# A Hyena, S5 and ConvGLU block: transfers moved, x normalised in two halves, gate sums in 16 steps

## The chip, the cores and the metric

One core of one Trainium2 chip. The metric is the device time of one execution in microseconds (us). The engines are named as in the profile: PE (matrix products), DVE (vector), ACT (activation), POOL (general), SP (here it only issues transfers).

## The reference

One layer (DEPTH 1, D_MODEL 1024, 1024 tokens, a context of 256 tokens) in fp32:

```
pc = modulated_norm(ctx, norm_g[l, 0], mod_c[0], mod_c[1]) @ w_in[l]
yc_s5, ctx_state = s5_mixer(pc[..., h_split:], *s5_args, None, not last)

px = modulated_norm(x, norm_g[l, 0], mod_x[0], mod_x[1]) @ w_in[l]
yx_s5, _ = s5_mixer(px[..., h_split:], *s5_args, ctx_state, True)
yx_hy = hyena_mixer(px[..., :h_split], *hyena_args)
yx = jnp.concatenate([yx_hy, yx_s5], axis=-1) @ w_out[l]
x = x + mod_x[2] * rms_norm(yx, norm_g[l, 1])
hx = modulated_norm(x, norm_g[l, 2], mod_x[3], mod_x[4])
x = x + mod_x[5] * rms_norm(conv_glu_ffn(hx, rows, *ffn_args), norm_g[l, 3])
```

The six rows of `mod_x` are `silu(c) @ w_ada + b_ada`: shifts, scales and gates of 1024 columns each. `hyena_mixer` is a short convolution, a long convolution by FFT (four channel tiles of 128 here) and a gate. `s5_mixer` is a bidirectional diagonal state space model whose output passes a GELU and then a GLU, `y * sigmoid(y @ w_glu + b_glu)`.

## The kernel before

Nearly all products keep fp32 precision as three products of split operands (`mm3`, lines 228 to 230). A scheduler orders PE, DVE and ACT, except where program order is pinned; transfers issued by SP (`ld`, line 152) keep program order, POOL's work too. Lines 143, 149 and 161 are helpers that record DVE's and POOL's two-operand operations and ACT's activations, so instructions of many places carry them.

**Start, 0 to 48 us.** Eight steps k multiply the conditioning by the first two rows of `w_ada` (`ada_mm`, line 308), 1 MB each. From step 4 on each also squares one of the four tiles `xr` of x (two token blocks each) on ACT, with a sum per token. After the loop `norm(2, 8)` turns the eight sums into factors (a square root on ACT, small DVE instructions) and `apply` scales the four tiles on DVE. The row of products is copied (`mrow`), transposed on PE (line 592), and DVE makes the coefficients `AB`, `A0` of it. `k_load(0)` and `ld(Cb)` load tables; the first filter taps are products at line 445.

**Projections of x, to 204 us.** `Cc[1]` is negated on ACT as soon as its table `k_c` has come. `w_split(i)` splits weight tiles into a high and a low part, `x_cols(k)` transposes x on PE (line 648) and applies scale and shift on ACT (the high part), then DVE (the low part), and `x_mm` multiplies.

**S5 turns, 204 to 432 us and beyond.** A loop over n = 0 to 8 does S5 batch n in pieces (`s5_u`, `s5_gt`, `s5_kc`, `s5_e`, `s5_scan_a`, `s5_toep`, `s5_scan_b` for turn n, `s5_out` for n−1). Between the pieces `hy_next` does pieces of the Hyena projections and `sums_next(MS[i])` steps of the generator `gate_sums`: the remaining four rows of `w_ada`, in steps of 128 columns. One step loads 512 KB into the single buffer `wm`, issues eight narrow products into a PSUM bank (line 691, 32 output partitions), copies them to SBUF on ACT, sums partitions with a short product (line 693), and adds the bias on ACT. After each row's last step `gate_end` makes the scale, or transposes the row and writes it to memory `g_d`. `MS = (1, 2, 2, 1, 1)` gives seven steps a turn, and four in the last.

**End of S5, 500 to 614 us.** The long convolution of channel tile ct is `u_spec(ct)` (forward FFT, PE and DVE), `product(ct)` with the filter's spectrum `kf` on DVE, and `inverse(ct)`: `fft_inv` on DVE, products with the table `idft` on PE (line 1078), and the gate on DVE. The S5 output was written to memory `ys_d` by ACT's queue and is read back as `ys4`, in another layout. The GLU (`glu_w`, `glu_y`, `glu_high` at line 1187, `glu_low` at line 1195) works on pairs of 128 output channels: a sigmoid on ACT into the one buffer `sg`, a multiplication by it on DVE. Then come `inverse(1)` to `inverse(3)`, and `wo_load`, `wo_split`: `w_out`, whose products begin at 613.5 us. The FFN follows.

Of the kernel before, what the change touches and what calls it, by code (L numbers as in the profile page):

```python
# [108 lines left out]
def hybrid_block(ctx: ExitStack, tc: tile.TileContext, t, out):  # L109
# [19 lines left out]
    def FRing(n, *dims, at=None):  # L129
        return Ring(sa, n, *dims, at=at)  # L130
# [29 lines left out]
    def act(o, i, f, **k):  # L160
        return pin(A, A.activation(o, i, f, **k))  # L161
# [355 lines left out]
    def norm(o, n):  # L517
        rstd(nrs[:, o:o + n], nss[:, o:o + n], ntmp[:, :, o:o + n])
# [61 lines left out]
    norm(2, 8)  # L580
    for q in range(4):
        apply(V, xr[q], 2 + 2 * q)
# [76 lines left out]
    def gate_end(i, b0):  # L659

        if i == 4:
            stt(V, A2, SB2[:, 1], 1.0, g2v, ADD, MUL)
        if i in (2, 5):
            z = 2 + (i == 5)
            tt(V, SB2[:, z], SB2[:, z], g13[:, z - 2], MUL)
            PE.transpose(PS[:8, b0, 0:128], SB2[:, z], ident)
            act(macc[:8], PS[:8, b0, 0:128], AF.Copy)
            ld(g_d[z - 2][0].rearrange("(k c) -> k c", k=8), macc[:8])
# [3 lines left out]
    def gate_sums(gates, wm, acc, b0):  # L672

        steps = [(i, h) for i in gates for h in range(8)]
        ws_ = {}

        def load(n):
            if n < len(steps):
                i, h = steps[n]
                ws_[n] = wm.next()  # L680
                c0 = i * 1024 + 128 * h
                ld(ws_[n].rearrange("p (k c) -> p k c", k=8),
                   w_ada[:, c0:c0 + 128].rearrange("(k p) c -> p k c", p=128))

        load(0)
        for n, (i, h) in enumerate(steps):
            w = ws_.pop(n)
            w3_ = w.rearrange("p (k c) -> p k c", k=8)
            for k in range(8):
                j = k % 4  # L690
                PE.matmul(PS[32 * j:32 * j + 32, b0[0], 0:128], lhsT=cond[:, k], rhs=w3_[:, k], start=k < 4, stop=k >= 4)  # L691
            act(acc, PS[:, b0[0], 0:128], AF.Copy)
            PE.matmul(PS[:, b0[0], 128:130], lhsT=acc, rhs=sel, start=True, stop=True)
            z, bias = {3: (0, b34[:, 0:8]), 4: (1, b34[:, 8:16]), 2: (2, b25[:, 0:8]), 5: (3, b25[:, 8:16])}[i]
            act(SB2[:, z, h:h + 1], PS[:, b0[0], 128:129], AF.Identity, bias=bias[:, h:h + 1])
            if h == 7:
                gate_end(i, b0[0])
            load(n + 1)
            yield

    g_d = [drp.tile([1, 1024], F32, name=f"g{i}_d") for i in range(2)]
    macc = F(128, at=(0,))
# [37 lines left out]
    act(Cc[1], Cc[1], AF.Copy, scale=-1.0)  # L740
    w_split(0)
    x_cols(0)
    for k in range(8):
        i = k // 2
        if k % 2:
            w_split(i + 1)
        if k < 7:
            x_cols(k + 1)
        disc_next(D0[k])
        k_next(K0[k])  # L750
        x_mm(i, k, 0)
# [5 lines left out]
    sums = gate_sums((3, 4, 2, 5), wm, macc, gb)  # L757
# [39 lines left out]
    for k in range(8):  # L797
# [4 lines left out]
        sums_next(M_WIN)  # L802
# [229 lines left out]
    s5_load(0)  # L1032

# [49 lines left out]
    for n in range(9):  # L1083
# [5 lines left out]
        if n == 5:  # L1089
            sums_next(48)  # L1090
            wm.put()
            sa.put(macc)
# [71 lines left out]
    graw, sg = F(2, 512, at=(7,)), F(1024, at=(7,))  # L1164
    xin = FRing(2, 1024, at=(7,))
# [65 lines left out]
    sa.put(graw, sg, yh, *yl, *gw)  # L1231
# [242 lines left out]
MS, UF = (1, 2, 2, 1, 1), 1  # L1474
# [107 lines left out]
```

## Time and profile before

| what | before |
|---|---|
| runs | 1447.63 us median of 3 (1445.07 to 1448.21) |
| profiled execution | 1447.4 us, its span 1445.6 us |
| PE busy | 1326.1 us (92%), 6668 instructions |
| DVE busy | 883.5 us (61%), 1208 instructions |
| ACT busy | 482.3 us (33%), 802 instructions |
| POOL busy | 472.5 us (33%), 250 instructions |
| mean granted clock of PE | 0.951 |
| moved by DMA | 144.48 MB, mean 100 GB/s |

The span runs from the first to the last instruction of the profiled execution. Idle time in a row stands in brackets with what ended it. PE's instructions overlap: one product of 512 columns lasts 0.39 us in the rows, and the next begins 0.23 us after it.

### The profile page before, as it was taken

Reading aid. Unit: us, or ns where it says so; the run is one execution under the profiler, and the core shown is the slowest. Engines: PE = TensorE matmul, PEld = TensorE weight load, DVE = VectorE, ACT = ScalarE, POOL = GpSimd, SP = SyncE. Lnnn points to the kernel's source line nnn. Section 1 sums busy time; section 2 is a strip of 40 time slices with the busy share of each in tenths; the row PEclk is TensorE's granted clock in tenths of the full one; section 3 lists DMA queues with packets and bytes.
Section 4 is the critical chain, followed back from the end, with each engine's and each line's share of the span. In section 5 each row is a group of like instructions: output and inputs, shape, how many; then the busy total and the mean of one; then the engine's idle time right before and its main releaser. Section 6 shows DMA issues by size and latency. Waiting matters only on the chain.

```text
span 1445.6 us, 16905 instructions
## 1 busy us (share of the span) xinstructions
PE 1326.1 (92%) x6668; PEld 1071.5 (74%) x6668; DVE 883.5 (61%) x1208; ACT 482.3 (33%) x802; POOL 472.5 (33%) x250
## 2 busy tenths in 40 slices
PE   4888789899989957899999999999999999999997
PEld 0666567677767855787778888888888888888886
DVE  7776842456677999647766755755756757115314
ACT  3632122444433413346633222222222233224321
POOL 0000726556589203210122222222222226443540
PEclk8799899989998887999999999999999999999999
DMA  9423143545533225213311111111111115335422
GB/s 376 143 96 102 66 94 93 163 138 154 156 94 109 74 83 209 73 58 114 124 44 44 49 54 44 46 57 44 45 57 44 44 58 171 107 101 176 132 73 88
DMA packets 149639, 144.48 MB, mean 100 GB/s; under 512 B 29860, under 2 KB 128696, under 8 KB 147128
## 3 DMA queue, kind: packets, MB, share of 16 engines
q1 hardware_dynamic: 135000, 124.67, 27.9%
q10 hardware_dynamic: 14560, 18.74, 3.7%
q8 instruction: 52, 0.85, 0.2%
q14 instruction: 27, 0.22, 0.1%
HBM read 123.98 MB, written 19.37 MB: 99 GB/s over the span
## 4 chain that ended last, share of the span: by engine, by line
PE 73%; DVE 16%; DMA 5%; ACT 3%; issue 2%; SPq 1%; ACTq 0%; DVEq 0%
PE PS L228 21%; PE PS L229 21%; PE PS L230 21%; DVE s L143 12%; ACT s L161 3%; DMA s<-in_w_ada_dram 2%; DVE s L149 1%; PE PS L691 1%; PE PS L972 1%; DVE s L1001 1%; PE PS L428 1%; DMA s<-in_x_dram 1%; PE PS L936 1%; PE PS L429 1%; PE PS L1078 1%
## 5 line engine op out<-in xcount | busy, mean ns | idle before, releaser
L228 PE MATMUL PS<-s,s 128*128 128x512 f32 x1320 | 527.6, 401 | 4.2 <-ACT s L161 3.9
L229 PE MATMUL PS<-s,s 128*128 128x512 f32 x1320 | 524.1, 397 | 0.0
L230 PE MATMUL PS<-s,s 128*128 128x512 f32 x1320 | 523.1, 397 | 0.1
L161 ACT ACTIVATE s<-s 128x512 fp32r<-128x512 f32 (+9 forms) x356 | 259.6, 748 | 641.0 <-PE PS L229 208.2
L143 POOL TENSOR_TENSOR s<-s,s 128x1024 fp32r<-128x1024 f32 x98 | 252.2, 2577 | 613.5 <-ACT s L161 593.5
L143 DVE TENSOR_TENSOR s<-s,s 128x512 fp32r<-128x512 f32 (+6 forms) x178 | 196.8, 1117 | 218.7 <-ACT s L161 210.4
L143 POOL TENSOR_TENSOR s<-s 128x512 f32<-128x512 f32 (+2 forms) x147 | 219.0, 1503 | 262.4 <-PE PS L445 145.7
L228 PEld LDWEIGHTS PS<-s,s 128*128 128x128 f32 x1320 | 258.2, 196 | 59.9 <-ACT s L161 6.4
L230 PEld LDWEIGHTS PS<-s,s 128*128 128x128 f32 x1320 | 258.0, 196 | 53.8 <-issue 2.7
L229 PEld LDWEIGHTS PS<-s,s 128*128 128x128 f32 x1320 | 258.8, 196 | 52.5 <-issue 2.6
L149 DVE SCALAR_TENSOR_TENSOR s<-s,s 128x1024 f32<-128x1024 f32 x140 | 218.0, 1557 | 102.5 <-ACT s L161 98.3
L143 DVE TENSOR_TENSOR s<-s 128x512 f32<-128x512 f32 (+11 forms) x403 | 187.0, 500 | 41.9 <-DMA s<-s 27.1
L161 ACT ACTIVATE s<-PS 128x512 f32<-128x512 f32 (+6 forms) x212 | 110.8, 538 | 227.1 <-PE PS L429 53.2
L149 DVE SCALAR_TENSOR_TENSOR s<-s 128x1024 f32<-128x1024 f32 (+5 forms) x136 | 107.6, 807 | 54.9 <-ACT s L161 52.5
L161 ACT ACTIVATE s<-PS,s 128x128 f32<-128x128 f32 (+5 forms) x161 | 101.9, 680 | 81.7 <-PE PS L230 18.5
L143 DVE TENSOR_TENSOR s<-PS,s 128x512 f32<-128x512 f32 (+3 forms) x81 | 52.4, 668 | 62.5 <-ACT s L161 24.4
L230 PE MATMUL PS<-s 128*128 128x512 f32 x136 | 53.7, 395 | 0.0
L228 PE MATMUL PS<-s 128*128 128x512 f32 x136 | 53.4, 395 | 0.0
L229 PE MATMUL PS<-s 128*128 128x512 f32 x136 | 53.4, 392 | 0.0
L149 DVE SCALAR_TENSOR_TENSOR s<-PS,s,s 128x1023 f32<-128x1023 f32 x24 | 30.6, 1278 | 26.4 <-ACT s L161 25.9
L1078 PE MATMUL PS<-s,s 128*128 128x256 f32 x128 | 31.2, 406 | 15.6 <-DMA s<-in_k_idft_dram 14.8
L1078 PEld LDWEIGHTS PS<-s,s 128*128 128x128 f32 x128 | 26.1, 205 | 20.2 <-DVE s L143 16.1
(89 smaller groups left out, 803.0 us busy)
## 6 DMA issues: line engine op xcount, KB each, us to landing
s<-in_ffn_w_up_dram SPq DMA_DIRECT2D x44, 512.0 KB
s<-in_ffn_w_down_dram SPq DMA_DIRECT2D x44, 512.0 KB
s<-in_w_ada_dram SPq DMA_DIRECT2D x32, 512.0 KB
s<-in_w_in_dram SPq DMA_DIRECT2D x20, 512.0 KB
s<-in_w_ada_dram SPq DMA_DIRECT2D x8, 1024.0 KB
s<-in_x_dram SPq DMA_DIRECT2D x4, 1024.0 KB
kf_d<-s ACTq DMA_DIRECT2D x4, 1024.0 KB
s<-kf_d SPq DMA_DIRECT2D x4, 1024.0 KB
```

What stands on the lines that cost most here:

```text
L143: return pin(e, e.tensor_tensor(o, a, b, op=op))
L149: return pin(e, e.scalar_tensor_tensor(o, a, s, b, op0=op0, op1=op1))
L161: return pin(A, A.activation(o, i, f, **k))
L228: PE.matmul(dst, lhsT=hi, rhs=mh, start=first, stop=False)
L229: PE.matmul(dst, lhsT=hi, rhs=ml, start=False, stop=False)
L230: PE.matmul(dst, lhsT=lo, rhs=mh, start=False, stop=last)
L428: PE.matmul(o, lhsT=dft[:, c, r], rhs=hkb[:, r, 0], start=True, stop=False)
L429: PE.matmul(o, lhsT=dft[:, 2 * c, r2], rhs=hkb[:, r2, 1], start=False, stop=True)
L691: PE.matmul(PS[32 * j:32 * j + 32, b0[0], 0:128], lhsT=cond[:, k], rhs=w3_[:, k], start=k < 4, stop=k >= 4)
L936: PE.matmul(pk_[:, g], lhsT=d["G"][:, z, g * 128:(g + 1) * 128], rhs=CC[z][:, g].rearrange("p d q -> p (d q)"), start=z == 0, stop=z == 1)
L972: PE.matmul(PS[h:h + 64, bk, i * 160:(i + 1) * 160], lhsT=d["GT"][:, z, g * 128 + h:g * 128 + h + 64], rhs=u, start=True, stop=True)
L1078: PE.matmul(bk[:, 256 * j:256 * j + 256], lhsT=zb[:, k, c], rhs=idft[:, 2 * h + j, i], start=i == 0, stop=i == 3)
```

## The change

1. The norm of x is done in halves: after steps k = 5 and k = 7 a norm of four sums, and the scaling of the two tiles that they belong to.
2. The negation of `Cc[1]` on ACT stands after `x_cols(4)`, in place of ahead of the first `w_split`.
3. `gate_sums` takes two steps (256 columns) a visit, in 16 visits. Each step's weights come in two loads of 256 KB; two views hold one step each. A visit first finishes the visit before (two short products, one addition of the bias on DVE), then does 16 narrow products, one copy on ACT, and issues the next four loads. `gate_end`'s transposition uses other columns of the bank, and a buffer of its own. `MS = (1, 1, 1, 0, 1)`: four visits a turn.
4. At the end of S5 the loads stand in another order, and `idft` is loaded in two halves. The two GLU weight tiles have a buffer each.
5. The scheduler's order of PE, DVE and ACT follows.

```
             sums_sq(xr[k - SQ0], 2 + 2 * (k - SQ0), PS[:, 2:4].rearrange("p a b -> p (a b)"))
-    norm(2, 8)
-    for q in range(4):
-        apply(V, xr[q], 2 + 2 * q)
+            if (k - SQ0) % 2:
+                h = k - SQ0 - 1
+                norm(2 + 2 * h, 4)
+                for q in (h, h + 1):
+                    apply(V, xr[q], 2 + 2 * q)
...
-            PE.transpose(PS[:8, b0, 0:128], SB2[:, z], ident)
-            act(macc[:8], PS[:8, b0, 0:128], AF.Copy)
-            ld(g_d[z - 2][0].rearrange("(k c) -> k c", k=8), macc[:8])
+            PE.transpose(PS[:8, b0, 384:512], SB2[:, z], ident)
+            act(grow_[:8], PS[:8, b0, 384:512], AF.Copy)
+            ld(g_d[z - 2][0].rearrange("(k c) -> k c", k=8), grow_[:8])
...
-                ld(ws_[n].rearrange("p (k c) -> p k c", k=8),
-                   w_ada[:, c0:c0 + 128].rearrange("(k p) c -> p k c", p=128))
+                for u in range(2):
+                    ld(ws_[n][u].rearrange("p (k c) -> p k c", k=4),
+                       w_ada[512 * u:512 * u + 512, c0:c0 + 128].rearrange("(k p) c -> p k c", p=128))
...
+        load(1)
+        def finish(n):
+            i, h = steps[n]
+            for m in range(2):
+                PE.matmul(PS[:, b0[0], 256 + 2 * m:258 + 2 * m], lhsT=acc[:, 128 * m:128 * m + 128], rhs=sel, start=True, stop=True)
             z, bias = {3: (0, b34[:, 0:8]), 4: (1, b34[:, 8:16]), 2: (2, b25[:, 0:8]), 5: (3, b25[:, 8:16])}[i]
-            act(SB2[:, z, h:h + 1], PS[:, b0[0], 128:129], AF.Identity, bias=bias[:, h:h + 1])
-            if h == 7:
+            tt(V, SB2[:, z, h:h + 2], PS[:, b0[0], 256:260:2], bias[:, h:h + 2], ADD)
+            if h == 6:
                 gate_end(i, b0[0])
-            load(n + 1)
+
+        for n in range(0, len(steps), 2):
+            if n:
+                finish(n - 2)
+            for m in range(2):
+                w3_ = [w.rearrange("p (k c) -> p k c", k=4) for w in ws_.pop(n + m)]
+                for k in range(8):
+                    j = k % 4
+                    PE.matmul(PS[32 * j:32 * j + 32, b0[0], 128 * m:128 * m + 128], lhsT=cond[:, k], rhs=w3_[k // 4][:, j],
+                              start=k < 4, stop=k >= 4)
+            act(acc, PS[:, b0[0], 0:256], AF.Copy)
+            load(n + 2)
+            load(n + 3)
             yield
+        finish(len(steps) - 2)
+        yield
...
-    act(Cc[1], Cc[1], AF.Copy, scale=-1.0)
     w_split(0)
     x_cols(0)
...
+        if k == 3:
+            act(Cc[1], Cc[1], AF.Copy, scale=-1.0)
...
+    w2_ = [F(512, at=(2,)), F(512, at=(8,))]
+    macc, grow_ = F(256, at=(2, 8)), F(128, at=(0, 2, 8))
+    wmv = Views([[wm.b[0][:, 0:512], wm.b[0][:, 512:1024]], w2_])
+    sums = gate_sums((3, 4, 2, 5), wmv, macc, gb)
...
-    graw, sg = F(2, 512, at=(7,)), F(1024, at=(7,))
+    graw, sg = [T(2, 512) for _ in range(2)], F(1024, at=(7,))
...
-        ld(graw, t["s5_w_glu"][0, 256 * h:256 * h + 256].rearrange("(k p) c -> p k c", p=128))
...
+    for h in range(2):
+        ld(graw[h], t["s5_w_glu"][0, 256 * h:256 * h + 256].rearrange("(k p) c -> p k c", p=128))
+    kf_load(3)
+    wo_load(4)
+    wo_load(5)
+    for h in range(2):
+        ld(idft[:, 2 * h:2 * h + 2], t["k_idft"][:, 2 * h:2 * h + 2])
     ld(ys4, ys_d.rearrange("k p c -> p k c"))
-    ld(idft, t["k_idft"])
     glu_w(0)
     glu_w(1)
-    wo_load(4)
-    wo_load(5)
-    kf_load(3)
...
-MS, UF = (1, 2, 2, 1, 1), 1
+MS, UF = (1, 1, 1, 0, 1), 1
```

Three pieces of the order show it. SP's queue at the end of S5, as a difference (s_0_71 is the segment that holds `idft`, s_1_2941 and s_1_2948 the one that holds `kf`):

```order
-L152 DMA s_1_2941<-kf_d 128x2048
-L152 DMA s_2_2940<-uT_d 128x1024
+L152 DMA s_1_2948<-kf_d 128x2048
+L152 DMA s_2_2947<-uT_d 128x1024
+L152 DMA s_0_65<-in_s_w_glu_dram 128x2x512 x2
+L152 DMA s_1_2948<-kf_d 128x2048
+L152 DMA s_0_65<-in_w_out_dram 128x1024 x2
+L152 DMA s_0_71<-in_k_idft_dram 128x2048 x2
 L152 DMA s_0_65<-ys_d 128x4x1024
-L152 DMA s_0_71<-in_k_idft_dram 128x4096
-L152 DMA s_0_65<-in_s_w_glu_dram 128x2x512 x2
-L152 DMA s_0_65<-in_w_out_dram 128x1024 x2
-L152 DMA s_1_2941<-kf_d 128x2048
```

All of these loads now stand ahead of the load of ys, which waits for the stores of the last turn.

PE's queue at one step of the gate sums in a steady turn, before:

```order
L229 MATMUL PS<-s_0_302,s_1_300 128x512
L691 MATMUL PS<-s_0_67,s_0_64 32x128 [waits DMAHW7_49,Activation_49]
L691 MATMUL PS<-s_0_67,s_0_64 32x128 x7
L230 MATMUL PS<-s_1_301,s_1_300 128x512
L228 MATMUL PS<-s_1_301,s_1_300 128x512
L229 MATMUL PS<-s_0_302,s_1_300 128x512
L693 MATMUL PS<-s_0_64 128x2 [waits Activation_49]
L230 MATMUL PS<-s_1_301,s_1_300 128x512
```

and at one visit in the change (the last narrow products of the visit are left out):

```order
L230 MATMUL PS<-s_1_308,s_1_307 128x512
L693 MATMUL PS<-s_0_64,s_0_68 128x2 [waits Activation_49]
L693 MATMUL PS<-s_0_64,s_0_68 128x2
L925 MATMUL PS<-s_0_64,s_0_68 128x32 [waits DMAHW3_49]
L925 MATMUL PS<-s_0_64,s_0_68 128x32 x3
L934 MATMUL PS<-s_0_64,s_0_68 128x128 [waits Pool_49]
L934 MATMUL PS<-s_0_64,s_0_68 128x128 x2
L706 MATMUL PS<-s_0_67,s_0_64 32x128 [waits DMAHW1_49,DVE_49]
L706 MATMUL PS<-s_0_67,s_0_64 32x128 x3
L706 MATMUL PS<-s_0_67,s_0_64 32x128 [waits DMAHW2_49]
```

The short products stand ahead of a visit's narrow ones (L706 is the line of the narrow products in the change), and the first narrow product waits for DVE where it waited for ACT.

DVE's queue in one turn of the change, with one addition of the bias (the row of 128x2) behind a block of the scan:

```order
L143 TENSOR_TENSOR s_0_70<-s_0_70,s_0_68 128x1024 [waits DVE_49]
L992 MEMSET s_0_65 128x4 [waits Activation_49]
L143 TENSOR_TENSOR s_0_70<-s_0_70 128x4x128 [waits DVE_49]
L143 TENSOR_TENSOR s_0_70<-s_0_70,s_0_68 128x1024 [waits DVE_49]
L143 TENSOR_TENSOR s_0_70<-s_0_70 128x4x128 [waits DVE_49]
L143 TENSOR_TENSOR s_0_64<-PS,s_0_64 128x2 [waits PE_49,Activation_49]
L143 TENSOR_TENSOR s_1_307<-s_0_65,s_1_307 128x1024 [waits DMAHW4_49,Activation_49]
```

The program before has no such row: its bias is added on ACT.

## Rows read from the trace of the kernel before

**Rows 1.** The page's section 4: shares of the chain that ended last, by engine.
```profile
PE 73%; DVE 16%; DMA 5%; ACT 3%; issue 2%; SPq 1%; ACTq 0%; DVEq 0%
```

**Rows 2.** Stretches: span, busy time (instructions) of each engine, PE clock, DMA share, GB/s.
```profile
288.00:306.00 18.00, 15.38 (x100) 11.29 (x100) 15.46 (x15) 6.68 (x18) 6.54 (x5) 0.62 0.50 139
306.00:408.00 102.00, 98.71 (x790) 74.08 (x789) 54.76 (x51) 45.87 (x100) 68.03 (x46) 1.00 0.54 156
...
540.00:552.00 12.00, 1.24 (x3) 1.09 (x4) 10.57 (x13) 3.92 (x5) 0.00 (x0) 0.50 0.94 388
552.00:576.00 24.00, 21.91 (x81) 17.44 (x81) 23.86 (x28) 8.66 (x10) 13.18 (x4) 0.84 0.44 154
...
615.00:1446.00 831.00, 818.59 (x3611) 672.53 (x3609) 458.44 (x505) 262.86 (x400) 229.88 (x91) 0.99 0.25 77
```

**Rows 3.** Chain of waits, start of the program: start us, us, what.
```profile
39.12 8.46 DMA s<-in_k_c_dram
```

**Rows 4.** Timeline, 36 to 52 us: start, us, instructions, [idle before <-what ended it].
```profile
38.95 1.28 ACT L161 ACT_TABLE_LOAD   x1
...
41.53 5.39 DVE L146 TENSOR_SCALAR s<-s,s 128x1024 f32<-128x1024 f32 x8
...
46.84 0.19 DVE L143 TENSOR_TENSOR s<-PS,s 128x32 f32<-128x32 f32 x1
...
47.25 3.62 PE L445 MATMUL PS<-s 128*128 128x512 f32 x4
47.60 1.57 ACT L161 ACTIVATE s<-s 128x512 f32<-128x512 f32 x2 [5.90 <-DMA s<-in_k_c_dram]
...
49.08 3.44 ACT L161 ACTIVATE s<-PS,s 128x512 fp32r<-128x512 f32 x5
```

**Rows 5.** Groups by line, PE, 208 to 432 us: busy us, mean ns of one.
```profile
L691 PE MATMUL PS<-s,s 128*32 128x128 f32 x512 | 21.9, 292 | 5.0 <-DMA s<-in_w_ada_dram 4.6
...
L693 PE MATMUL PS<-s 128*128 128x2 f32 x64 | 11.3, 247 | 0.6 <-ACT s L161 0.6
```

**Rows 6.** PE's waits, 200 to 440 us: us in total, times, longest.
```profile
PE PS L691 <- DMA s<-in_w_ada_dram: 4.6, 6, 1.2
```

**Rows 7.** Chain of waits, 260 to 300 us.
```profile
270.85 4.98 DMA s<-in_w_ada_dram
...
282.35 0.23 PE PS L228
```

**Rows 8.** Timeline of DVE, 408 to 432 us.
```profile
419.57 5.42 DVE L1001 TENSOR_TENSOR_SCAN s<-s,s 128x640 f32<-128x640 f32 x2
```

**Rows 9.** Chain of waits, 528 to 620 us.
```profile
535.69 2.26 DMA ys_d<-s
...
538.21 7.50 DMA s<-ys_d
```

**Rows 10.** Timeline of PE, 536 to 616 us.
```profile
550.76 9.85 PE L1078 MATMUL PS<-s,s 128*128 128x256 f32 x32 [14.85 <-DMA s<-in_k_idft_dram]
...
584.04 3.44 PE L1187 MATMUL PS<-s 128*128 128x512 f32 x8 [3.96 <-ACT s L161]
...
592.78 9.66 PE L1078 MATMUL PS<-s,s 128*128 128x256 f32 x44
603.18 10.63 PE L1078 MATMUL PS<-s,s 128*128 128x256 f32 x48 [0.74 <-DVE s L143]
```

**Rows 11.** Timelines of DVE in short windows from 543 to 600 us.
```profile
543.26 2.35 DVE L143 TENSOR_TENSOR s<-s 128x1024 f32<-128x1024 f32 x2
...
547.04 4.63 DVE L143 TENSOR_TENSOR s<-s,s 128x1024 fp32r<-128x1024 f32 x4 [1.43 <-ACT s L161]
...
564.45 8.66 DVE L143 TENSOR_TENSOR s<-s 128x256 f32<-128x256 f32 x6
...
579.15 9.44 DVE L143 TENSOR_TENSOR s<-s 128x512 f32<-128x512 f32 x12
```

**Rows 12.** Timeline of ACT, 536 to 630 us.
```profile
582.87 1.11 ACT L161 ACTIVATE s<-PS,s 128x1024 f32<-128x1024 f32 x1 [7.99 <-DVE s L143]
```

More of the change, by code (lines that the diff above doesn't have):

```diff
@@ L127, in R, with FRing @@
         return sa.get(*dims, dt=F32R, at=at)
-    def FRing(n, *dims, at=None):
-        return Ring(sa, n, *dims, at=at)
+    def FRing(n, *dims, **kw):
+        return Ring(sa, n, *dims, **kw)
     def RRing(n, *dims, at=None):
@@ L681, in load @@
                 c0 = i * 1024 + 128 * h
-                ld(ws_[n].rearrange("p (k c) -> p k c", k=8),
-                   w_ada[:, c0:c0 + 128].rearrange("(k p) c -> p k c", p=128))
+                for u in range(2):
+                    ld(ws_[n][u].rearrange("p (k c) -> p k c", k=4),
+                       w_ada[512 * u:512 * u + 512, c0:c0 + 128].rearrange("(k p) c -> p k c", p=128))
         load(0)
[L686 to L693, printed above, removed]
+        load(1)
[3 more added lines that the diff above has]
+                PE.matmul(PS[:, b0[0], 256 + 2 * m:258 + 2 * m], lhsT=acc[:, 128 * m:128 * m + 128], rhs=sel, start=True, stop=True)
             z, bias = {3: (0, b34[:, 0:8]), 4: (1, b34[:, 8:16]), 2: (2, b25[:, 0:8]), 5: (3, b25[:, 8:16])}[i]
-            act(SB2[:, z, h:h + 1], PS[:, b0[0], 128:129], AF.Identity, bias=bias[:, h:h + 1])
-            if h == 7:
+            tt(V, SB2[:, z, h:h + 2], PS[:, b0[0], 256:260:2], bias[:, h:h + 2], ADD)
+            if h == 6:
                 gate_end(i, b0[0])
-            load(n + 1)
+        for n in range(0, len(steps), 2):
[10 more added lines that the diff above has]
+            load(n + 3)
             yield
+        finish(len(steps) - 2)
+        yield
     g_d = [drp.tile([1, 1024], F32, name=f"g{i}_d") for i in range(2)]
-    macc = F(128, at=(0,))
     gb = [3]
@@ L756, in hybrid_block @@
     ld(ctx_t, ctx_d.rearrange("(i p) c -> p i c", p=128))
-    sums = gate_sums((3, 4, 2, 5), wm, macc, gb)
     sums_sq(ctx_t, 0, vj)
@@ L801, in hybrid_block @@
         nxt = ctx_cols(k + 1) if k < 7 else None
-        sums_next(M_WIN)
         if k in TE:
@@ L1091, in hybrid_block @@
             wm.put()
-            sa.put(macc)
+            sa.put(macc, grow_, *w2_)
             yh2 = F(2, 1024, at=(1,))
@@ L1163, in hybrid_block @@
     ysT = [ys4[:, i] for i in range(4)]
-    graw, sg = F(2, 512, at=(7,)), F(1024, at=(7,))
-    xin = FRing(2, 1024, at=(7,))
+    graw, sg = [T(2, 512) for _ in range(2)], F(1024, at=(7,))
+    xin = FRing(2, 1024, at=(7,), top=True)
     idft = F(4, 4, 256, at=(8,))
@@ L1170, in glu_w @@
     def glu_w(h):
-        ld(graw, t["s5_w_glu"][0, 256 * h:256 * h + 256].rearrange("(k p) c -> p k c", p=128))
         k2 = slice(2 * h, 2 * h + 2)
-        act(gw[0][:, k2], graw, AF.Copy)
-        tt(G, gw[1][:, k2], graw, f32(gw[0][:, k2]), SUB)
+        act(gw[0][:, k2], graw[h], AF.Copy)
+        tt(G, gw[1][:, k2], graw[h], f32(gw[0][:, k2]), SUB)
     def glu_y():
@@ L1230, in hybrid_block @@
                 f(n + m, 2 * m)
-    sa.put(graw, sg, yh, *yl, *gw)
+    sa.put(*graw, sg, yh, *yl, *gw)
     r_a = RRing(4, 2, 4, 128, at=(2,))
```

## The prediction

> **What bounds the kernel now.** I read the chain of waits first. PE holds 73% of it and DVE 16% [rows 1]: what takes time off PE's queue counts almost everywhere, and what takes time off DVE counts in a few stretches. The table by stage names the stretches. From 615 us to the end PE is busy 818.59 of 831 us at clock 0.99 [rows 2]; the change touches nothing there, so whatever is gained earlier arrives at the end undiminished, and so is whatever is lost. Three stretches ahead of it are touched. At the start, the chain waits for a transfer, k_c, ahead of the first projections [rows 3]. In the S5 turns (204 to 432 us) PE is nearly full: 98.71 of 102 us between 306 and 408, with one bad hole, 288 to 306, where it ran at clock 0.62 [rows 2]. And between 540 and 552 us PE worked 1.24 of 12 us while the DMA engines were busy 94% of the time [rows 2]: PE waits there for one table.
>
> **Start (x in halves, the negation of Cc).** What sets the end is ACT's first high part of the normalised x, at 49.08 us [rows 4]. It stands behind the negation of Cc[1], which waited for its transfer until 47.57 [rows 3] and shares 1.57 us with the high part of the weights [rows 4]. With the negation at k = 3 that wait is gone from the path (0.55 us of work stays on ACT, later, beside PE's products). What is late next is the inputs of x_cols(0). Now one norm of 8 columns follows the last square, behind a table load of 1.28 us, and eight scalings of DVE last from 41.53 to 46.92; the coefficients, on DVE behind them, come at 46.84 [rows 4]. With halves the table load and four scalings (2.7 us) lie before the last squares; the second norm lacks the 1.28 us, and its own four scalings end near 43.2; the transposed coefficients then come near 45.1. So the first high part moves from 49.1 to about 45.3: −3.8 us. Against that, the four passes of the filter taps, which stood in PE's hole (3.62 us there, [rows 4]), now stand behind 24 products: some 1.0 us at the pace of a full PE. Six small DVE instructions are new, in DVE's idle. I take **−2.8**; bounds −4.5 (the taps stay covered) and 0 (the next transfer or the squares hold the path).
>
> **Gate sums.** Per column PE now has 16 narrow passes (L691) and 2 short ones (L693), 21.9 and 11.3 us over 32 steps [rows 5]. Narrow passes stay. Short ones become bunches of four: between no gain and half of 11.3 us; I take −3, since part of the 247 ns each is the change of shape, once per bunch now. The wait of the short product for ACT's copy goes, since it comes a visit later; the trace has too little of it to count. ACT loses 48 small instructions; it has idle there, so nothing.
>
> The transfers: twice the bytes per visit, at half as many visits. A load of 512 KB stood on the chain for 4.98 us, the first of five such stretches of 4.2 to 5.0 [rows 7]; PE idled 4.6 us for loads in all [rows 6], the rest lay beneath other PE work. The four half-column buffers come free as a visit's narrow passes read them, and the next 1 MB cannot land much under 5 us later. Counting the order of the change at 0.23 us a product pass [rows 7], three of the four gaps of a turn hold about 5 to 6 us of PE work and the fourth 18 to 20, shorter in the first turns. So some gaps fall short by a microsecond, as now: bounds −4.6 and +9, taken at 0.
>
> A new wait comes in. The bias add moves from ACT to DVE, and the next narrow product, in the same bank, waits for it; between a visit's short products and that narrow product stand only 0.7 to 1.3 us of PE rows. Behind the narrow product queues all of PE. DVE is busy half of the time (54.76 of 102 us, in 51 pieces of 1.07 us mean, [rows 2]; the longest, scans while POOL works, 2.7 us, [rows 8]). Half a piece, half of the time, makes 0.25 us for each of 15 visits: +3.6. Bounds 0 and the first rival below. In the slow hole at 288 to 306 us PE lost 2.6 us idle and, at clock 0.62, more in the passes [rows 2]; it may heal or move, and I count neither. Gates: −3 + 0 + 3.6, rounded to **0**, from −9 to +9.
>
> **End of S5 (freed transfers).** Before, the 2 MB of the inverse table are queued behind the load of ys, which waits for the last store (2.26 us, then 7.50 for the load, [rows 9]). inverse(0) on PE waits 14.85 us for them and starts at 550.76 [rows 10], though DVE's inverse FFT had finished by 543.4, when it goes on to the next tile [rows 11]. In the change the table is issued ahead of ys: the first half waits for DVE's last read of the old tenant (about 526), the second for PE's last S5 products (533). At the rate of 540 to 552, 388 GB/s [rows 2], 1 MB takes 2.7 us; both halves are there before 543. Then inverse(0) runs from 543.5 to about 553.4, a shift of −7.3. ys itself cannot land earlier than now.
>
> What follows is late by other things. The four low parts of y start at 547 as before; but DVE no longer fills the next 8 us with inverse FFTs of later tiles: it takes the products of inverse(0) between them, then the fourth forward FFT (part of the row of 8.66 us for six instructions, [rows 11], stretched while POOL worked), its spectrum product, and sg0. PE's first GLU pair ends near 565.5, sg0 on DVE near 569.7. In the trace ACT's second sigmoid, which needs sg0 done, ran only at 582.87, 7.99 us late [rows 12], and PE waited 3.96 for it [rows 10]. So the second pair ends near 579 instead of 592.5, and 92 inverse passes at 0.22 us, which run to 613.8 now [rows 10], end near 600: −13. DVE must still do all of its work: from 543.4 to 588.6 it was busy for 43.8 us [rows 11]. Postponed, that and the four sg products end near 590, with half of PE's passes left, so it does not quite set the end. Allowing for gaps on DVE while it waits for inverse(0), I take **−12.5**; bounds −16 and −3 (DVE full throughout, the second rival).
>
> The Trainium skill, "DMA: Bandwidth & Descriptors", section "Issuing engines are not separate DMA queues", speaks against this part: transfers started from different engines still share the same 16 DMA engines. By it the last ys stores, from ACT's queue, would share with the table's second half from SP's; the sum would be some 2 us less good. No row here shows the two together.
>
> **Sum.** −2.8 + 0 − 12.5 = −15.3 us against the profiled execution's 1447.4: **1432 us**. That execution lies 0.2 us under the median of the runs, 1447.63, so the forecast against it is the same within rounding. About 0.2%, 2.9 us, is what a measurement of this kernel can tell from no change.
>
> **Rivals.**
> 1. *PE waits for DVE at the visits* (the other side). Place: the first narrow product of 15 visits. If the add stands behind a whole scan pair while POOL works (two took 5.42 us, [rows 8]), one visit costs 2.7 us; 15 cost 40, in place of 3.6, and the time is about 1469. It decides from 1.25 us a visit on (18.9/15). For: in the order of the change several adds stand behind the last multiplication of a scan block, after which nothing frees PE. Against: other adds stand between short operations, and DVE idles 46% there [rows 2]. Chance 0.10. The Trainium skill, "PSUM — Partial Sum Buffer", section "PSUM bank collisions raise a hardware error", says that two engines must be kept apart by bank and quadrant, even on different columns: by it the wait cannot be left out. The order of both programs agrees.
> 2. *DVE holds the end stretch.* It was busy 23.86 of 24 us between 552 and 576 [rows 2], and the change removes none of its work. If the postponed inverse FFTs end as late as before plus the three sg products (3.6 us), the last 48 passes (10.63 us, [rows 10]) follow near 600: −3 in place of −12.5, about 1441. Against: after 588.6 DVE waited for sigmoids, and PE had 92 passes in stock. Chance 0.14.
> 3. *The loads of 1 MB do not fit the gaps*: 12 short gaps by 0.75 us, +9: about 1441. For: the waits for loads that are there now [rows 6, 7]. Chance 0.09.
> 4. *The hole heals too*: −2.6 of idle, and some 4 us of slow passes of 288 to 306 us, and the end gives its −16: about 1420. Chance 0.10.
> 5. *The halves or the order do nothing*: no case here, since the order of the change shows each of them.
>
> **How the numbers follow.** The forecast has 0.57, its own range 1425 to 1439. The range of 8 in 10 takes in the second and third rivals above and most of the fourth below: **1417 to 1443**; it leaves out the first and the tails. Faster by over 0.2%: 0.55 of the forecast, 0.12 and 0.07 of rivals 2 and 3, 0.10 of the fourth: 0.84. Slower: 0.10. Within: 0.06.
>
> **What would show it.** Right: in the profile after, ACT's first high part near 45; inverse(0) starting at 543 to 544 less the 3 us gained before; no wait of PE for the inverse table; the second GLU pair ending 13 us sooner, and PE full from there. Each line of waits of narrow products on DVE should sum under 6 us. Wrong: a sum of such waits over 19 us; an inverse table that lands after DVE's inverse FFT; the last inverse passes waiting for DVE.

## The result, and the profile after

The changed kernel takes 1430.38 us (median of 4 runs, 1427.59 to 1434.97), the kernel before 1447.92 us beside it: a ratio of 0.9864, 95% interval 0.9837 to 0.9890. The forecast was 1432, the range 1417 to 1443. The profiled execution of the change took 1431.79 us, its span 1430.0, 15.6 us less than before. The total came out as forecast; its terms did not, so that the hit is in good part luck. Five instructions that both programs have, in their start times (us):

| mark | before | after | difference | gained since the mark above |
|---|---|---|---|---|
| first product of the projections (L228) | 51.23 | 47.76 | −3.5 | 3.5 |
| last product of the filter tables (L428) | 195.5 | 194.2 | −1.3 | −2.2 |
| first scan of turn 5 (DVE) | 448.11 | 438.89 | −9.2 | 7.9 |
| last scan (DVE) | 514.06 | 503.14 | −10.9 | 1.7 |
| first product of w_out (L228) | 613.46 | 599.45 | −14.0 | 3.1 |
| end of the span | 1445.6 | 1430.0 | −15.6 | 1.6 |

So the start kept 1.3 us (forecast 2.8), the S5 turns gained 9.6 (forecast 0), and the end of S5 3.1 (forecast 12.5). The last 1.6 us lie behind `w_out`, where the change touches nothing: in the kernel before PE ran there at half clock once, from 726.9 to 730.3 us. Seven of the fourteen profiles of this document have such a stretch there, whatever their edit; that of the change has none.

Of the page of the change, busy time by engine and the shares of the chain, which answer to [rows 1] and the table ahead of the prediction: PE is busy 9 us less, DVE 7 us more.

```profile
PE 1317.4 (92%) x6668; PEld 1071.5 (75%) x6668; DVE 890.7 (62%) x1230; ACT 471.7 (33%) x755; POOL 479.9 (34%) x250
...
PE 72%; DVE 15%; DMA 6%; ACT 3%; issue 2%; POOL 2%; SPq 0%; ACTq 0%; DVEq 0%; POOLq 0%
```

The stretches of the change at the times of [rows 2] (columns as there; the work in them stands earlier by what was gained):

```profile
288.00:306.00 18.00, 14.54 (x130) 10.62 (x128) 16.24 (x15) 8.99 (x18) 11.65 (x7) 0.91 0.49 142
306.00:408.00 102.00, 97.69 (x731) 78.78 (x722) 64.42 (x63) 36.79 (x66) 70.09 (x45) 0.98 0.43 126
...
540.00:552.00 12.00, 6.87 (x17) 4.44 (x17) 12.00 (x12) 4.77 (x7) 5.82 (x2) 0.65 0.28 89
552.00:576.00 24.00, 24.00 (x104) 19.87 (x104) 22.78 (x30) 6.59 (x6) 4.78 (x2) 0.96 0.05 15
```

Of the hole at 288 to 306 us the idle time is still there (14.54 busy of 18), the low clock is not: 0.91 where it was 0.62. Between 540 and 552 us DVE is now busy for all of the 12 us, and POOL beside it for 5.82.

PE's waits of the change, 190 to 440 us, answer to [rows 6], and its groups of lines, 195 to 432 us, to [rows 5]:

```profile
PE PS L706 <- DVE s L143: 8.8, 5, 3.5
...
PE PS L706 <- DMA s<-in_w_ada_dram: 1.4, 3, 0.8
```

```profile
L706 PE MATMUL PS<-s,s 128*32 128x128 f32 x512 | 20.9, 283 | 10.3 <-DVE s L143 8.8 <-DMA s<-in_w_ada_dram 1.4
...
L693 PE MATMUL PS<-s,s 128*128 128x2 f32 x64 | 8.9, 243 | 0.7 <-ACT s L161 0.7
```

The new wait for DVE is there, 8.8 us of it, while the wait for loads fell from 4.6 to 1.4 us, and the short products (L693) from 11.3 to 8.9.

At the start, ACT's first high parts and PE's first product, which answer to [rows 4], then PE's wait for DVE at the filter tables (timelines of the change):

```profile
45.49 4.12 ACT L161 ACTIVATE s<-PS,s 128x512 fp32r<-128x512 f32 x6 [2.86 <-DMA s<-in_k_dec_dram]
...
47.76 0.78 PE L228 MATMUL PS<-s,s 128*128 128x512 f32 x1
...
97.03 0.79 PE L428 MATMUL PS<-s 128*128 128x128 f32 x2 [4.85 <-DVE s L143]
```

and the same wait in the kernel before:

```profile
97.39 0.79 PE L428 MATMUL PS<-s 128*128 128x128 f32 x2 [4.85 <-DVE s L143]
```

Between the first product and that wait, the chain of the change goes through the passes of the filter taps (L445), which stood ahead of the first product before, to ACT's next high parts; the last line is ACT's row in the chain of the kernel before:

```profile
57.20 1.72 PE PS L445 x4
...
59.39 2.79 ACT s L161 x4
```

```profile
59.87 2.79 ACT s L161 x4
```

At the end of S5, the chain of the change answers to [rows 9], PE's timeline to [rows 10], DVE's to [rows 11]:

```profile
525.43 4.60 DMA ys_d<-s
530.08 7.54 DMA s<-ys_d
```

```profile
530.67 10.17 PE L1094 MATMUL PS<-s,s 128*128 128x256 f32 x32 [5.04 <-DVE s L143]
...
572.73 6.20 PE L1094 MATMUL PS<-s,s 128*128 128x256 f32 x28
583.56 16.24 PE L1094 MATMUL PS<-s,s 128*128 128x256 f32 x64 [4.62 <-DVE s L143]
```

```profile
538.73 4.86 DVE L143 TENSOR_TENSOR s<-s,s 128x1024 fp32r<-128x1024 f32 x2 [4.04 <-ACT s L161]
...
544.51 2.39 DVE L143 TENSOR_TENSOR s<-s,s 128x1024 fp32r<-128x1024 f32 x1
546.83 1.28 DVE L143 TENSOR_TENSOR s<-s 128x512 f32<-128x512 f32 x2
548.03 1.21 DVE L143 TENSOR_TENSOR s<-s,s 128x1024 fp32r<-128x1024 f32 x1
...
560.48 10.57 DVE L143 TENSOR_TENSOR s<-s 128x512 f32<-128x512 f32 x13
572.26 10.22 DVE L143 TENSOR_TENSOR s<-s 128x1024 f32<-128x1024 f32 x5 [1.22 <-ACT s L161]
```

and POOL's timeline:

```profile
531.23 14.59 POOL L143 TENSOR_TENSOR s<-s,s 128x1024 fp32r<-128x1024 f32 x4 [57.41 <-DVE s L143]
```

PE no longer waits for the inverse table: inverse(0) starts as soon as DVE is done. But three of the four low parts of y, beside POOL, take 2.4 us each, and the fourth 1.21, where all four took 4.63 in [rows 11]; and of the last 92 inverse passes 64 wait for DVE.

Of the whole stretch from the last scan to the first product of `w_out`, before and after (columns as in [rows 2]):

```profile
514.10:613.50 99.40, 69.89 (x311) 59.07 (x311) 86.44 (x101) 27.29 (x31) 23.40 (x8) 0.83 0.32 114
```

```profile
503.10:599.50 96.40, 74.59 (x311) 62.67 (x311) 86.21 (x101) 26.93 (x31) 25.87 (x8) 0.81 0.33 114
```

PE's idle time falls from 29.5 to 21.8 us, but its passes take 4.7 us more, at a lower granted clock.

### The profile page after: what moved, and what is told of

The parts are those of the page before. It is cut to its first block, busy times and chain, and to the rows that moved or that the text cites. A ratio compares the mean times of both kernels' runs of the same rounds, so it can differ in the third digit from the quotient of the medians.

```text
span 1430.0 us, 16933 instructions
## 1 busy us (share of the span) xinstructions
PE 1317.4 (92%) x6668; PEld 1071.5 (75%) x6668; DVE 890.7 (62%) x1230; ACT 471.7 (33%) x755; POOL 479.9 (34%) x250
## 4 chain that ended last, share of the span: by engine, by line
PE 72%; DVE 15%; DMA 6%; ACT 3%; issue 2%; POOL 2%; SPq 0%; ACTq 0%; DVEq 0%; POOLq 0%
PE PS L228 21%; PE PS L229 21%; PE PS L230 21%; DVE s L143 11%; ACT s L161 3%; DMA s<-in_w_ada_dram 2%; POOL s L143 2%; DVE s L149 2%; PE PS L1094 1%; DVE s L1013 1%; DMA s<-in_k_dec_dram 1%; PE PS L1202 1%; PE PS L428 1%; PE PS L429 1%; PE PS L948 1%
## 5 line engine op out<-in xcount | busy, mean ns | idle before, releaser
L228 PE MATMUL PS<-s,s 128*128 128x512 f32 x1320 | 527.2, 401 | 3.3 <-ACT s L161 3.2
L161 ACT ACTIVATE s<-s 128x1024 fp32r<-128x1024 f32 (+10 forms) x357 | 259.9, 746 | 669.4 <-PE PS L229 224.0
L143 DVE TENSOR_TENSOR s<-s,s 128x512 fp32r<-128x512 f32 (+6 forms) x178 | 202.9, 1149 | 189.3 <-ACT s L161 180.7
L143 POOL TENSOR_TENSOR s<-s 128x512 f32<-128x512 f32 (+2 forms) x147 | 223.7, 1535 | 249.7 <-PE PS L445 142.8
L228 PEld LDWEIGHTS PS<-s,s 128*128 128x128 f32 x1320 | 257.7, 196 | 58.3 <-ACT s L161 4.9
L229 PEld LDWEIGHTS PS<-s,s 128*128 128x128 f32 x1320 | 258.3, 196 | 53.7 <-issue 3.2
L230 PEld LDWEIGHTS PS<-s,s 128*128 128x128 f32 x1320 | 257.7, 196 | 53.6 <-issue 1.9
L161 ACT ACTIVATE s<-PS 128x512 f32<-128x512 f32 (+5 forms) x196 | 106.9, 567 | 197.5 <-PE PS L429 51.0
L161 ACT ACTIVATE s<-PS,s 128x128 f32<-128x128 f32 (+4 forms) x129 | 94.0, 784 | 74.3 <-PE PS L230 21.3
L143 DVE TENSOR_TENSOR s<-PS,s 128x512 f32<-128x512 f32 (+4 forms) x97 | 54.7, 582 | 91.5 <-PE PS L693 29.2
L228 PE MATMUL PS<-s 128*128 128x512 f32 x136 | 53.4, 395 | 0.0
L143 DVE TENSOR_TENSOR s<-s,PS 128x1024 f32<-128x1024 f32 x21 | 25.6, 1221 | 23.7 <-ACT s L161 23.7
```

The source lines that it names most:

```text
L143: return pin(e, e.tensor_tensor(o, a, b, op=op))
L228: PE.matmul(dst, lhsT=hi, rhs=mh, start=first, stop=False)
L229: PE.matmul(dst, lhsT=hi, rhs=ml, start=False, stop=False)
L230: PE.matmul(dst, lhsT=lo, rhs=mh, start=False, stop=last)
```

## The experiments

**One part alone.** Three kernels put one part each into the kernel before. `e1_start`: the norm in halves and the negation of Cc. Its edit:

```
-    norm(2, 8)
-    for q in range(4):
-        apply(V, xr[q], 2 + 2 * q)
+            if (k - SQ0) % 2:
+                h = k - SQ0 - 1
+                norm(2 + 2 * h, 4)
+                for q in (h, h + 1):
+                    apply(V, xr[q], 2 + 2 * q)
...
-    act(Cc[1], Cc[1], AF.Copy, scale=-1.0)
...
+        if k == 3:
+            act(Cc[1], Cc[1], AF.Copy, scale=-1.0)
```

> The kernel before with parts 1 and 2 alone (norm in halves, negation of Cc at k = 3). By the forecast's term -2.8 us (about 1445.1); by the profile of the change, where the first product is 3.5 us earlier but the last product of the filter tables (L428) only 1.4 us, about -1.4 (1446.5). If it gives nothing, the 3.5 us were given back to DVE's table work completely.

Measured: 1453.41 us, ratio 1.0027 (1.0014 to 1.0040). Alone, the start makes the kernel slower, which neither number held.

`e2_gates`: the gate sums as in the change, everything else as before.

```
+        for n in range(0, len(steps), 2):
+            if n:
+                finish(n - 2)
...
-MS, UF = (1, 2, 2, 1, 1), 1
+MS, UF = (1, 1, 1, 0, 1), 1
```

> The kernel before with part 3 alone (gate sums in 16 visits). By the forecast's term 0 (between -9 and +9); by the profile of the change, where the S5 turns end 10.3 us earlier of which 1.4 are the start's, about -9 (1439). First rival: +15 or more, if PE's waits for the bias addition on DVE outweigh what the fewer visits save.

Measured: 1434.56 us, ratio 0.9903 (0.9886 to 0.9919). The gates alone carry 14 us, more than either number.

`e3_end`: the transfers at the end as in the change, everything else as before.

```
+    kf_load(3)
+    wo_load(4)
+    wo_load(5)
+    for h in range(2):
+        ld(idft[:, 2 * h:2 * h + 2], t["k_idft"][:, 2 * h:2 * h + 2])
     ld(ys4, ys_d.rearrange("k p c -> p k c"))
-    ld(idft, t["k_idft"])
...
```

> The kernel before with part 4 alone (order of the transfers at the end of S5, the inverse table in halves). By the forecast's term -12.5 (1435); by the profile of the change, where the stretch from the end of S5 to the first product of w_out is 76.5 us in place of 80.3, about -3.7 (1444), since DVE holds it. PE's wait for the inverse table should be gone in either case.

Measured: 1446.13 us, ratio 0.9979 (0.9967 to 0.9991): 3 us. Over the nine profiles with the new order of the transfers that leave POOL's work as it is, the first product of `w_out` follows the last scan after 95.6 to 97.5 us; over the three with the old order, after 99.4 to 100.6. In `e3_end` the last scan begins at 516.76 and the first product of w_out at 612.36, 95.6 us later, where it is 99.4 before. The wait for the inverse table is gone; PE's waits from 500 to 600 us show what is there instead:

```profile
PE PS L1078 <- DVE s L143: 9.7, 2, 5.1
...
PE PS L1186 <- DVE s L143: 5.4, 2, 4.2
```

9.7 + 5.4 us for DVE, in place of the 14.85 for the table [rows 10].

**The start left out.** `e5_no_start` is the change without the edit of `e1_start`.

```
+    norm(2, 8)
+    for q in range(4):
+        apply(V, xr[q], 2 + 2 * q)
...
```

> The changed kernel without parts 1 and 2 (one norm of 8 columns after the loop, the negation of Cc at its old place); gates and transfers as changed. If the start costs what it cost alone (+0.27%, 3.9 us), about 1426.5 against 1430.4 of the change; if it is worth the -1.4 us that the profile of the change shows at the filter tables, about 1432; if DVE's filter and table work gives it all back, 1430.4.

Measured: 1431.97 us, ratio 0.9882 (0.9863 to 0.9902): not to be told from the change, and just the product of the ratios of `e2_gates` and `e3_end`. The profiles say where the start's gain goes. Over ten profiles with halves and four without, the first product comes 3.6 us sooner with halves in the mean, the 25th product 1.3, the end of PE's wait at the filter tables 0.7; the last L428 begins at 193.5 to 196.0 us with halves, at 193.6 to 196.3 without. In `e3_end`, whose start is the old one, PE's wait for DVE at the filter tables (4.85 us) ends even sooner than in the change:

```profile
96.17 0.79 PE L428 MATMUL PS<-s 128*128 128x128 f32 x2 [4.85 <-DVE s L143]
```

Why the start alone costs 3.9 us is open. The order of the S5 turns is that of the kernel before, and no one wait there shows it. In its profile the stretch from the last L428 to the first scan of turn 5 takes 257.3 us, 5.2 more than before; but `e3_end`, with the same order and 256.6 us there, is faster than the kernel before.

**What in the gates pays.** `e4_bias_act` adds the bias on ACT again.

```
-            tt(V, SB2[:, z, h:h + 2], PS[:, b0[0], 256:260:2], bias[:, h:h + 2], ADD)
+            for m in range(2):
+                act(SB2[:, z, h + m:h + m + 1], PS[:, b0[0], 256 + 2 * m:257 + 2 * m], AF.Identity, bias=bias[:, h + m:h + m + 1])
```

> The changed kernel with the bias of each visit added on ACT again (two small activations in place of one DVE addition); nothing else. If the 8.8 us that PE waited for DVE at narrow products are lost time, about -5 to -9 against the change (1422 to 1426). If ACT's queue takes DVE's place, or the waits only stand where PE would have waited for the loads anyway, no difference (1430).

Measured: 1435.28 us, ratio 0.9908 (0.9882 to 0.9935). No gain; the interval overlaps that of the change. In its profile narrow products wait 11.7 us for ACT in place of 8.8 for DVE.

```profile
PE PS L707 <- ACT s L161: 11.7, 3, 4.7
```

`g1_same_visit` issues the short products in their own visit.

```
-            if n:
-                finish(n - 2)
...
             act(acc, PS[:, b0[0], 0:256], AF.Copy)
+            finish(n)
...
```

> The changed kernel with the short products, the bias addition and the end of a row issued in their own visit, right behind the copy on ACT, and not at the next visit. Theory that the halved number of visits pays and the next-visit issue does not: 1430 or less, down to 1422, since the 8.8 us that narrow products waited for DVE go. Theory that the next-visit issue pays: PE waits for ACT's copy in its place, as it did for 11.7 us with the bias on ACT, and the time is about 1435 or more.

Measured: 1441.82 us, ratio 0.9955 (0.9937 to 0.9972), 11.4 us above the change. The short products wait for ACT's copy:

```profile
PE PS L693 <- ACT s L161: 12.1, 4, 7.3
```

`g2_32_next` does the opposite: 32 visits of one column, but the short product at the next visit.

```
-        for n in range(0, len(steps), 2):
+        for n in range(len(steps)):
             if n:
-                finish(n - 2)
-            for m in range(2):
+                finish(n - 1)
+            for m in range(1):
...
-MS, UF = (1, 1, 1, 0, 1), 1
+MS, UF = (1, 2, 2, 1, 1), 1
```

> The changed kernel with 32 visits of one column again (MS as before, two columns loaded ahead), the short product and the bias still issued at the next visit, the bias on DVE. Theory that the next-visit issue carries the gain of the gates: 1429 to 1433. Theory that both are needed (half the visits, half the changes of shape on PE): 1436 to 1442, as the same-visit run with 16 visits gave 1441.8. More visits that wait for DVE could make it slower still.

Measured: 1436.99 us, ratio 0.9922 (0.9909 to 0.9935), 6.6 us above the change: leaving out either half of the idea costs, and the next visit more. In `e4_bias_act`, `g1_same_visit`, `g2_32_next` and `c1_banks` the scheduler also put PE's instructions of the turns in another order, so that each of them measures its edit with that order. The stretch from the last L428 to the first scan of turn 5, in `g1_same_visit` (its profiled execution, 1447.62 us, is the slowest of its twelve) and in the change (columns as in [rows 2]):

```profile
196.10:450.80 254.70, 231.67 (x1643) 177.48 (x1643) 151.85 (x153) 89.35 (x163) 162.37 (x107) 0.91 0.45 126
```

```profile
194.60:438.90 244.30, 221.57 (x1622) 172.59 (x1621) 149.36 (x154) 87.50 (x162) 166.70 (x108) 0.94 0.47 131
```

PE's idle time is the same, 23.0 and 22.7 us. What differs is busy time, 231.7 and 221.6. In the traces the granted clock is 1.0 or 0.5 at any time, the two levels of 2.4 and 1.2 GHz; busy time times (1 − granted clock), summed over windows of 2 us, is then an estimate of what the lower level costs. It is 17.3 and 11.4 us, so 5.9 of the 10.1 us are passes at a lower clock. The other 4.2 are other work: of PE's instructions 1643 and 1622 fall into the stretch, since the scan that ends it stands elsewhere among them. Up to the last scan PE has done the same 2062 instructions in each of them (the rows count those at their edges too). The kernel before, the change and `g1_same_visit`:

```profile
195.80:514.10 318.30, 288.45 (x2067) 228.24 (x2065) 198.76 (x206) 126.70 (x264) 190.39 (x124) 0.92 0.44 126
```

```profile
194.50:503.10 308.60, 278.91 (x2065) 225.76 (x2063) 204.24 (x221) 115.89 (x215) 195.08 (x124) 0.94 0.45 131
```

```profile
196.10:517.30 321.20, 290.45 (x2065) 231.44 (x2064) 208.40 (x222) 116.67 (x215) 194.50 (x124) 0.90 0.44 126
```

| up to the last scan, us | idle | lost to the clock (estimate) | rest |
|---|---|---|---|
| before | 29.9 | 20.8 | 267.6 |
| change | 29.7 | 14.6 | 264.3 |
| `g1_same_visit` | 30.7 | 26.4 | 264.1 |
| `g2_32_next` | 30.5 | 19.1 | 266.0 |

In these profiles the next visit brings clock alone; half the visits bring 4.5 us of clock and 1.7 of the rest. The profiles that share an order of the turns bear it out: three with that of before (`e1_start` and `e3_end` beside it) lose 20.8 to 24.3 us to the clock, with a rest of 267.2 to 267.7; seven with that of the change (`e2_gates`, `e5_no_start` and four of the kernels below beside it) lose 14.0 to 16.3, with a rest of 263.2 to 264.3.

`c1_banks` takes the wait for DVE away: the short sums stand in other PSUM banks than the narrow products.

```
+            q = (5, 7, 7, 5)[(n // 2 + 1) % 4]
...
-                PE.matmul(PS[:, b0[0], 256 + 2 * m:258 + 2 * m], lhsT=acc[:, 128 * m:128 * m + 128], rhs=sel, start=True, stop=True)
+                PE.matmul(PS[:, q, 496 + 2 * m:498 + 2 * m], lhsT=acc[:, 128 * m:128 * m + 128], rhs=sel, start=True, stop=True)
...
```

> The changed kernel with the short sums of a visit in bank 5 or 7 (by slot of the turn, where their next use is furthest) in place of the gates' own bank 6; nothing else. Narrow products then wait for ACT's copy of the visit before, long done, and no more for DVE. If the 8.8 us of such waits are lost time: 1422 to 1426. If other instructions of PE wait for DVE in those banks instead, or the order that the scheduler makes costs more shape changes: 1429 or more.

Measured: 1433.48 us, ratio 0.9896 (0.9881 to 0.9910): no gain. The 8.8 us are gone, another wait grew, and the same stretch of this kernel reads

```profile
PE PS L923 <- ACT s L161: 5.0, 2, 4.2
```

```profile
193.50:438.17 244.67, 227.49 (x1625) 176.93 (x1624) 152.38 (x153) 87.30 (x162) 167.78 (x108) 0.92 0.49 131
```

17.2 us idle, 5.5 less than in the change, but 227.5 busy at clock 0.92, 16.1 us of it lost to the clock: in this profile lower clock took what the waits gave. The seven profiles with the change's order idle 19.8 to 22.7 us there and lose 10.6 to 11.8. Whether the removed wait or the new order of PE's instructions lowered the clock is not shown.

**What holds the end.** `f1_half_behind` issues the table's second half behind the load of ys.

```
-    for h in range(2):
-        ld(idft[:, 2 * h:2 * h + 2], t["k_idft"][:, 2 * h:2 * h + 2])
+    ld(idft[:, 0:2], t["k_idft"][:, 0:2])
     ld(ys4, ys_d.rearrange("k p c -> p k c"))
+    ld(idft[:, 2:4], t["k_idft"][:, 2:4])
```

> The changed kernel with the second half of the inverse table issued behind the load of ys. Theory that the last stores of ys shared the DMA engines with it (4.60 us on the chain in place of 2.26): ys comes 2.3 us sooner, and of this up to 2.3 us reach the end (1428). Theory that DVE holds the stretch in any case: no difference (1430.4). If the second half of inverse(0) then comes too late for DVE, slower by 1 to 3 us.

Measured: 1428.74 us, ratio 0.9867 (0.9846 to 0.9889): as the change. On the chain the last store now takes 2.17 us in place of 4.60, and the low parts of y start 2.3 us sooner after the last scan (33.3 against 35.6), but the first product of w_out follows that scan after 96.1 us, and after 96.3 in the change. DVE uses the 2.3 us up: two operations behind its third low part take 3.43 us, and 1.28 in the change. The store's row in the chain, and DVE's:

```profile
522.38 2.17 DMA ys_d<-s
```

```profile
541.50 3.43 DVE L143 TENSOR_TENSOR s<-s 128x512 f32<-128x512 f32 x2
```

`f2_pool_late` was to move POOL's work.

```
-    for k in (4, 5):
-        wo_split(k, (5,))
-        wo_load(k + 2)
...
+    inverse(3, 6)
+    for k in (4, 5):
+        wo_split(k, (5,))
+        wo_load(k + 2)
...
```

> The changed kernel with POOL's low parts of w_out 4 to 7 (and the loads they free) behind inverse(3) in program order. Theory that DVE holds the end of S5 and is slowed by POOL working beside it (low parts of y at 2.4 us each where they took 1.16 before; five additions in 10.2 us): DVE gets through 5 to 8 us sooner and the time is 1423 to 1426. Rival: PE waits for w_out's low parts instead, 1430 or more.

Measured: 1428.95 us, ratio 0.9865 (0.9845 to 0.9886). It settles nothing of what it was for: no other work of POOL or SP stands between the old and the new place, so every engine has the order of the change. It serves as a repeat, and its stretch, 96.4 us, is the change's.

`f4_no_pool` takes the work away: it leaves out the low parts of w_glu and of w_out 4 to 7.

```
-        tt(G, gw[1][:, k2], graw[h], f32(gw[0][:, k2]), SUB)
+        act(gw[1][:, k2], graw[h], AF.Copy)
...
+        if k >= 4:
+            act(wo[k][:, 0], wo_raw[k], AF.Copy)
+            act(wo[k][:, 1], wo_raw[k], AF.Copy)
...
```

> The changed kernel in which the low parts of w_glu and of w_out 4 to 7 are not computed: ACT copies the raw values in their place, so POOL has nothing to do between the S5 turns and w_out 0 to 3; the values of GLU and output change, the number of products doesn't. Theory that POOL's work stretches DVE's there: low parts of y at 1.2 us each where three took 2.4, five operations of DVE behind the sigmoid in some 5 to 6 us where they took 10.2; the first product of w_out follows the last scan after 88 to 91 us where it took 96.3, and the time is 1422 to 1425. Rival: DVE's operations keep their lengths, 1429 to 1430.

Measured: 1422.89 us, ratio 0.9826 (0.9808 to 0.9844), 7.5 us below the change, and 6.1 below the median of the nine runs of the change and of its repeat `f2_pool_late`. Its first product of w_out begins at 589.29, 87.3 us after its last scan (502.02). DVE's two first low parts of y take 2.36 us in place of 4.86, and behind the spectrum product it does 18 operations in one go, in 15.19 us, where the change took 10.57 for thirteen and, after a gap of 1.22, 10.22 for the other five:

```profile
536.86 2.36 DVE L143 TENSOR_TENSOR s<-s,s 128x1024 fp32r<-128x1024 f32 x2 [3.28 <-ACT s L161]
...
554.94 15.19 DVE L143 TENSOR_TENSOR s<-s 128x512 f32<-128x512 f32 x18
```

That POOL stretches DVE here is shown by this run.

**A version that keeps the computation.** `c2_dve_lows`:

```
-        tt(G, gw[1][:, k2], graw[h], f32(gw[0][:, k2]), SUB)
+        tt(V, gw[1][:, k2], graw[h], f32(gw[0][:, k2]), SUB)
...
-        split(wo[k], wo_raw[k], G)
+        split(wo[k], wo_raw[k], V if k in (6, 7) else G)
```

> The changed kernel with the low parts of w_glu and of w_out 6 and 7 computed on DVE in place of POOL (the whole computation is kept). DVE has 4 us idle ahead of the low parts of y, where the two of w_glu fit; POOL's remaining low parts (w_out 4 and 5) then end before the low parts of y begin. By the run without POOL (1422.9): three operations on y get 1.2 us shorter each, five behind the first sigmoids lose some 5 us and get 2.4 us of new work: about 1424 to 1426, below both kernels. Rival: the four operations only add to a full DVE (4.8 us) and POOL's others contend as before: 1430 to 1433.

Measured: 1424.67 us, ratio 0.9846 (0.9832 to 0.9859), the fastest here that computes everything; the change's interval, 0.9837 to 0.9890, overlaps it, the four runs being spread, and so does that of `f2_pool_late`. Its trace gives the reason: DVE does the low parts of w_glu ahead of those of y, POOL is done by 533, and the four low parts of y take the 4.62 us of before:

```profile
528.54 5.68 DVE L143 TENSOR_TENSOR s<-s,s 128x1024 fp32r<-128x1024 f32 x2 [0.90 <-ACT s L161]
...
536.55 4.62 DVE L143 TENSOR_TENSOR s<-s,s 128x1024 fp32r<-128x1024 f32 x4
```

```profile
524.88 8.26 POOL L143 TENSOR_TENSOR s<-s,s 128x1024 fp32r<-128x1024 f32 x2 [53.43 <-ACT s L161]
```

From its last scan (500.77) to the first product of w_out (590.39) it takes 89.6 us, where the nine profiles that leave POOL's work as it is take 95.6 to 97.5. That stretch, more than the time of the whole, shows the gain.

## Why the prediction was right, and where it was not

The time and the sign were right, the size by luck: two wrong terms made up for each other, and a third was too large. Of the signs that it named, one of being wrong came (the last inverse passes wait for DVE), and one of being right failed (the waits of narrow products for DVE sum to 8.8 us, over 6).

*Start, −2.8.* The path was read rightly up to PE: the first high part came at 45.5, as worked out, and the first product 3.5 us sooner. The step that failed is the price of what PE does next, "some 1.0 us at the pace of a full PE". The four passes of the taps take 1.72 us behind the 24 products. And PE does not have the full pace: its granted clock is 0.50 until 52.1 us, so that the products and transpositions up to ACT's high parts at 59.4 us take another 1.3 us longer than before, where the clock had risen at 51.1, just ahead of the first product. Of the 3.5 us, 0.5 were left at 59.4 and 0.4 at the filter tables in the profile of the change. Taken out of the change, the start makes no difference that can be told; alone, it cost 3.9 us.

*Gate sums, 0.* The parts that were costed came out nearly so: short products −2.4 (−3; each still takes 243 ns, so that a price of the change of shape is not shown), loads −3.2 (0), waits for DVE +8.8 (+3.6, first rival's mechanism at half of its 1.25 us a visit). What failed is what was left uncounted: "it may heal or move, and I count neither". Up to the last scan the profile of the change gains 6.2 us in passes at a higher granted clock, 3.3 in the rest of PE's busy time, the short products among it, and 0.2 in idle time. Much of the clock lies in the hole: between 288 and 306 us, by the rows, 15.38 × (1 − 0.62) = 5.8 us are lost before and 14.54 × (1 − 0.91) = 1.3 in the change. What decides the grant is not shown here; the sum of PE's idle time does not, as it is the same. With the short products left in their own visit the time is 11.4 us longer, with 32 visits 6.6; that is more than the 14 us of the gates together, so the two overlap. Rival 4 had the mechanism, with 6.6 us and a chance of 0.10, but in one hole alone; its "some 4 us of slow passes" are 5.8 by the row, and its terms add up to 1422, not 1420.

*First rival.* Its wait appeared, and took 8.8 us of idle time. But it isn't a price by itself: the wait can be left out, with another bank, and the time is then no shorter (`c1_banks`, 1433.48 us), nor with ACT in DVE's place (1435.28).

*End, −12.5.* The forecast for PE held: no wait for the table, inverse(0) right behind DVE, the second GLU pair done 20.1 us sooner in absolute time (572.9 against 592.9), 9.1 of it since the last scan. The step that failed is "so it does not quite set the end". DVE does: −3.1 in the change, −3.0 alone, as the second rival had it (−3). It lacked the reason. Moved ahead, w_glu and w_out let POOL start its low parts at 531 and not at 553, beside DVE's low parts of y, which no row of before showed together, though the forecast named the stretching in two other rows; without POOL there, 6 to 7.5 us more come out. PE's passes, which the forecast took at full clock, lose 14.3 us to the clock in that stretch by the same estimate, and 9.2 before.

*Stores and table.* The last store took 4.60 us beside the table's second half, 2.17 without it. The Trainium skill, "DMA: Bandwidth & Descriptors", section "Issuing engines are not separate DMA queues", has transfers from different engines share the same DMA engines; by it the forecast gave some 2 us, and the trace agrees. The end moved by nothing in `f1_half_behind`, since DVE was late anyway.

## What to carry to other kernels

Short dependent products that stand alone on a full PE can cost more than their own time (here 11.3 us busy, 14 us gained): batch them, and issue each batch a visit later, when its operand has long been copied. Work that starts sooner gains less where PE has half its clock (1.3 of the 3.5 us at the start went so): read the granted clock of the stretch that it moves into. Before a transfer is moved earlier, see which engine it will wake, and what that engine will then run beside. A stage whose transfer wait is removed is worth only what the next full engine leaves; sum that engine's work over the whole stage, with its operations at the length that they have beside a busy neighbour.

## What the runs showed that was not expected

An idle time saved on PE was not time saved: `c1_banks`, with another order of PE's instructions, had 5.5 us less idle than the change and lost 4.7 us more of busy time to the granted clock. And three kernels with the same order of instructions in the S5 turns, the kernel before, `e1_start` and `e3_end`, took 252.1, 257.3 and 256.6 us from the last L428 to the first scan of turn 5 in their profiles: one profile does not price an edit of a few microseconds there.
